# A macaron layer in fp32 on one NeuronCore: the first feed-forward's copies and gates put in another order on ScalarE, row 7 turned a block later where feed-forward and attention meet, and the last block summed in two column halves

## The chip, the core and the metric

The kernel runs on one NeuronCore of a Trainium2 chip. The metric is the device time of one execution in microseconds (us), lower is better. The profile names the engines: PE is TensorE's matmul and PEld its weight load, ACT is ScalarE, DVE is VectorE, POOL is GpSimd, SP is SyncE, whose queue issues nearly all transfers.

## The reference, cut to what matters

The input is x with 1024 rows (tokens) of 1024 columns in fp32. DEPTH is 1, so only the layer with stick-breaking attention is there.

```python
def rms_norm(x, gain):
    y = x * lax.rsqrt(jnp.mean(x * x, axis=-1, keepdims=True) + 1e-6)
    return y * gain

def swiglu(xn, w_in, w_out):             # w_in 1024 x 5632, w_out 2816 x 1024
    gate, up = jnp.split(xn @ w_in, 2, axis=-1)
    return (jax.nn.silu(gate) * up) @ w_out

def reference(x, ...):
    x = x + 0.5 * swiglu(rms_norm(x, n1), w1_in, w1_out)
    x = x + stick_breaking_attention(rms_norm(x, gm), w_qkv, gq, gk, w_o)   # 16 heads of 64
    x = x + 0.5 * swiglu(rms_norm(x, n2), w2_in, w2_out)
    return x
```

## The kernel before, in words

**Split numbers.** Every product of two fp32 matrices is made from two parts of each operand. `split` (L196, L197) makes the high part on ACT by a Copy into fp32r and the low part on DVE or POOL by subtracting it. `mm3` (L308 to L310) then issues three matmuls into the same PSUM bank: high by high, high by low, low by high.

**Feed-forward, up.** `ffn_in` works through eleven pairs q of weight column blocks. A pair has a gate phase and an up phase; in each of them `seven` forms four 128 x 512 results from seven products (a Strassen form) of twelve matmuls each. The products go to the banks `ka`, `kc` and `kb` in the order ka, kc, kb, ka, kc, ka, kb. The bank `ka` is used three times in one phase and each use adds onto what stands there; in between, `copy` (L499, ACT) takes the bank's present content into a tile `s`, so PE may not start the second or the third use before the copy is done. `prepare` makes the seven weight operands of a phase: sums of weight blocks on DVE (`sf`, L475), then the splits by `unit` (tiles `u`), named a11, s1, a12, s2, s4, s3, a22. The operands of a phase are made about a phase ahead. After the gate phase four Silu activations run on ACT in place (`g`, L547), each behind the DVE sum that completes its tile (L503). For q = 2 alone the Silus are ordered behind the split of the gate phase's s3 (`marks["s3"]`, `following`). `following(mark)` only orders instructions of the mark's own engine; it adds no semaphore.

**Feed-forward, down.** `ffn_out` makes the second product from seven sums too, `SEVEN`: the products 5, 1, 4, 3, 7, 2, 6. Each takes four PSUM banks, `ma` or `mb`, one for each block t of 128 rows, and its operands come in six chunks loaded by SP (L361, L364), summed on DVE (L576) and split on ACT, DVE and POOL into tiles `rp`. Completed banks are added onto x on DVE (`result`, L622). The last product, 6, is summed block by block for its last three chunks (fifteen matmuls a block), so that finished rows can be used while PE sums the next block.

**The joint.** In the first feed-forward the blocks of product 6 are where the attention's input is made. `at` is called behind each block. `norm` scales a finished row (a row is 128 tokens here) on DVE into `xs` (L263), `turned` transposes it with eight matmuls of 128 columns into two banks (L287) and splits the two banks into `xh` and `xl`. Rows 4 to 7 are complete before product 6, rows 0 to 3 with its blocks 0 to 3. Behind block 0 the rows 6 and 7 are turned, sixteen matmuls, into mb0 to mb3, the banks of product 2, which DVE has to add onto x first. Row 0 is turned behind block 3, row 1 behind the first row of the QKV projection (bank `bt`, which lies where mb0 and mb1 were), rows 2 and 3 later. The rate of a row (its inverse root mean square) goes ACT square (L239), POOL sum and power (L248, L219, L220), and the row's scalings follow on DVE. Beside this ACT and POOL split the first QKV weights (`wqh`, `wql`, L948, L951). Two small POOL instructions (L946) hold the second half of these weights behind the last row turned, row 7 (`last_x`).

**The end.** The last block of the second feed-forward's product 6 is summed like every other one, added onto x on DVE and stored by SP (L1342).

**Order.** Each engine runs its instructions in the order of its queue. A list scheduler sets that order by the program's order and by the buffers; `following` (`tc.issue_after`) adds a constraint to it.

Of the kernel before, what the change touches and what calls it, by code (L numbers as in the profile page):

```python
# [17 lines left out]
P = 128  # L18
# [95 lines left out]
def macaron_kernel(ctx, tc, x, g1, w1_in, w1_out, gm, w_qkv, gq, gk, w_o, g2, w2_in, w2_out, out):  # L114
# [155 lines left out]
    def turned(xs, tb, bk, tl=None):  # L270
# [13 lines left out]
        for d in range(2):  # L284
# [5 lines left out]
            split(tp, xh[dst], xl[dst])  # L290
# [139 lines left out]
    def ffn_in(pl, w_in, keep, tl, hb, right, last):  # L430
# [35 lines left out]
        def prepare(raw, behind=None):  # L466
# [17 lines left out]
            us["s4"] = unit(pl, f["s4"], pool_e)  # L484
            mix("s3", a11, a21, ALU.subtract)
            us["s3"] = unit(pl, f["s3"], pool_e)
            marks["s3"] = marks["unit"]
# [6 lines left out]
        def seven(us, result):  # L494


            def copy(b):
                s = small(pl, "s")
                act.activation(s, b, AF.Copy)  # L499
                return s  # L500
# [13 lines left out]
            s2 = copy(a)  # L514
            product(c, us["s4"], b22, False)
# [11 lines left out]
        for q in range(1, NQ):  # L527
# [17 lines left out]
            for g in gs.values():  # L545
                with following(marks["s3"] if q == 2 else None):
                    act.activation(g, g, AF.Silu)  # L547

            us = prepare(stream(pl, w_in, q, 1), before[1, 1][:, 0:1] if q == 1 else None)
# [8 lines left out]
    def ffn_out(pl, w_out, keep, x_from, ahead, at):  # L558
# [37 lines left out]
        for m, tag, fresh, goes in SEVEN:  # L596
# [11 lines left out]
            def add(ts, cs):  # L608
                for c in cs:
                    (wh, wl), (hh, hl), _ = ops[c]  # L610
                    for i, q in enumerate(CHUNKS[c]):
                        for t in ts:
                            s = slice(t * P, (t + 1) * P)
                            mm3(
                                bs[t], [((hh[:, i, s], hl[:, i, s]), (wh[:, i], wl[:, i]))],
                                fresh and q == 0, q == NQ - 1, not fresh,
                            )

            def result(t, bs=bs, goes=goes):
                for (th, h), sign in goes:  # L620
                    xc = x_sb[h][:, 4 * (1 - th) + t, :]
                    dve.scalar_tensor_tensor(out=xc, in0=bs[t], scalar=0.5 * sign, in1=xc, op0=ALU.mult, op1=ALU.add)  # L622
# [7 lines left out]
            for t in range(4):  # L630
                add([t], range(n, len(CHUNKS)))
                if not late:
                    result(t)
                if last:
                    at(x_sb, m, f"block {t}", ops)
# [30 lines left out]
    with pools(*RAWS) as pr:  # L666
# [200 lines left out]
        with banks("ps2"), pools(*SECOND) as pl:  # L867
# [4 lines left out]
            def at(x_sb, m, where, ops):  # L872
# [25 lines left out]
                elif m == 6 and str(where).startswith("block"):  # L898
                    t = int(where[-1])
                    turn_rows("mb", (2, 0, 0, 1)[t])  # L900
                    squares(pn, row, (t,), half[:, t : t + 1], (1,))
                    last_norm = lambda: pending.extend(norm(pn, row, (t,), gain_m, half[:, t : t + 1], pooled=True))
                    if t < 3:
                        last_norm()
                    else:
                        late.append(last_norm)
# [9 lines left out]
    with ExitStack() as stack:  # L916
# [239 lines left out]
        last_x = ((pool_e, 0, lambda: xl[:, KD - 1, T - P : T - P + 1].bitcast(F32)),)  # L1156
# [170 lines left out]
    with banks("ps4"), pools(*SECOND) as pl:  # L1327
        lay_banks()

        def at(x_sb, m, where, ops):  # L1330
# [9 lines left out]
            for tb in tbs:  # L1340
                for h in hs:
                    sp.dma_start(out[rows(tb), HALVES[h]], x_sb[h][:, tb, :])  # L1342
# [42 lines left out]
```

## Time and profile before

| what | value |
|---|---|
| three runs | 1914.53, 1916.08, 1917.19 us |
| their median | 1916.08 us |
| the profiled execution | 1914.4 us |
| its span in the trace | 1912.5 us |
| PE busy | 1897.4 us (99%) |
| DVE, POOL, ACT busy | 1237.0, 1127.8, 979.9 us |
| bytes moved by DMA | 258.65 MB |

The span runs from the first to the last instruction of the trace; the time of the same execution is 1.9 us longer. A row of the timeline has the start in us from the span's start, the duration, engine, line, operation, tiles (out<-in), shapes and the count of merged instructions; in brackets stand the idle time before it and what ended that. A matmul's duration overlaps the next one's: the step from one start to the next is what counts on PE. A row of the waits has the waiting instruction, whom it waited for, the sum in us, the number of waits and the longest.

### The profile page before, as it was taken

To read this page: it belongs to the slowest core of one execution; us is meant where nothing else is said; L and a number is where in the kernel's file an instruction comes from. 1 tells how busy PE (TensorE), PEld (TensorE's weight loads), DVE (VectorE), ACT (ScalarE), POOL (GpSimd) and SP (SyncE) were. 2 spreads that over 40 slices of the span, in tenths; PEclk is the share of its full clock that TensorE was granted. 3 is DMA by queue.
4 is the path that set the end of the run, shared out by engine and by line. 5 is a ranking of instruction groups with operands and counts; after the bars stand their busy time and mean duration, and the time that the engine had idled before them with its cause. 6 is when DMAs were issued, how large, how long until landed. Compare 5 with 4: busy or idle time off the path is not lost.

```text
span 1912.5 us, 26698 instructions
## 1 busy us (share of the span) xinstructions
PE 1897.4 (99%) x9362; PEld 1624.8 (85%) x9362; DVE 1237.0 (65%) x1713; ACT 979.9 (51%) x1794; POOL 1127.8 (59%) x999
## 2 busy tenths in 40 slices
PE   9999999999999999999999999999999999999999
PEld 8878888888888899999999897788888888888887
DVE  6856445535775758888888777568456445548645
ACT  7433433334335458878888876344433443434332
POOL 6766666656556746656665564215666666654554
PEclk9999999999999999999999999999999999999999
DMA  6233323338897411011111152612333323369983
GB/s 204 89 115 111 105 87 117 105 115 278 307 354 259 138 34 45 32 47 45 45 37 42 50 170 74 225 50 74 103 110 116 105 83 117 110 229 342 331 268 138
DMA packets 168982, 258.65 MB, mean 135 GB/s; under 512 B 11664, under 2 KB 82320, under 8 KB 168848
## 3 DMA queue, kind: packets, MB, share of 16 engines
q1 hardware_dynamic: 168704, 256.95, 39.3%
q8 instruction: 73, 1.20, 0.3%
q14 instruction: 61, 0.50, 0.1%
q10 hardware_dynamic: 144, 0.00, 0.0%
HBM read 197.14 MB, written 59.77 MB: 134 GB/s over the span
## 4 chain that ended last, share of the span: by engine, by line
PE 86%; DVE 8%; ACT 3%; issue 1%; POOL 1%; DMA 0%; SPq 0%; DVEq 0%; ACTq 0%; POOLq 0%
PE ka L308 6%; PE ka L309 6%; PE ka L310 6%; PE bq L308 4%; PE bq L309 4%; PE bq L310 4%; PE kc L308 4%; PE kc L309 4%; PE kc L310 4%; PE ma L310 4%; PE ma L309 4%; PE ma L308 4%; PE kb L308 4%; PE kb L309 4%; PE kb L310 4%; PE mb L310 3%
## 5 line engine op out<-in xcount | busy, mean ns | idle before, releaser
L197 POOL TENSOR_TENSOR rp<-raw,rp 128x1024 fp32r<-128x1024 f32 x84 | 213.7, 2551 | 168.0 <-ACT rp L196 157.0
L197 POOL TENSOR_TENSOR u<-sf,u 128x512 fp32r<-128x512 f32 x160 | 227.6, 1425 | 136.2 <-ACT u L196 136.2
L197 POOL TENSOR_TENSOR u<-raw,u 128x512 fp32r<-128x512 f32 x128 | 187.5, 1467 | 152.5 <-ACT u L196 151.7
L196 ACT ACTIVATE u<-sf 128x512 fp32r<-128x512 f32 x160 | 100.8, 630 | 204.7 <-PE kb L309 87.1
L1073 POOL TENSOR_TENSOR w<-w,om 128x512 f32<-128x512 f32 (+4 forms) x128 | 140.9, 1104 | 107.6 <-DVE om L1066 94.0
L446 DVE TENSOR_TENSOR h<-h 128x512 f32<-128x512 f32 x110 | 135.4, 1234 | 85.8 <-POOL h L554 85.1
L308 PE MATMUL bq<-wqh,xh 128*128 128x384 f32 x512 | 174.4, 341 | 0.4
L196 ACT ACTIVATE rp<-rh 128x1024 fp32r<-128x1024 f32 (+1 forms) x78 | 76.4, 983 | 189.9 <-issue 60.2
L309 PE MATMUL bq<-wql,xh 128*128 128x384 f32 x512 | 172.2, 336 | 0.0
L310 PE MATMUL bq<-wqh,xl 128*128 128x384 f32 x512 | 172.1, 336 | 0.0
L576 DVE TENSOR_TENSOR raw<-raw 128x1024 f32<-128x1024 f32 (+1 forms) x60 | 95.0, 1585 | 105.4 <-DMA raw<-w_out 91.7
L196 ACT ACTIVATE u<-raw 128x512 fp32r<-128x512 f32 x128 | 80.2, 630 | 149.8 <-PE ka L309 100.8
L308 PE MATMUL ka<-xh,u 128*128 128x512 f32 x352 | 137.2, 390 | 1.9 <-ACT s L499 1.9
L308 PE MATMUL ma<-rp 128*128 128x512 f32 x352 | 137.0, 389 | 0.0
L310 PE MATMUL ka<-xh,u 128*128 128x512 f32 x352 | 137.0, 389 | 0.0
L310 PE MATMUL ma<-rp 128*128 128x512 f32 x352 | 136.9, 389 | 0.0
L309 PE MATMUL ka<-xl,u 128*128 128x512 f32 x352 | 136.9, 389 | 0.0
L309 PE MATMUL ma<-rp 128*128 128x512 f32 x352 | 136.9, 389 | 0.0
L554 POOL TENSOR_TENSOR h<-h,g 128x512 f32<-128x512 f32 x80 | 113.0, 1412 | 35.1 <-DVE h L503 33.3
L1062 ACT ACTIVATE w<-bz,f 128x512 f32<-128x512 f32 (+1 forms) x192 | 113.1, 589 | 34.5 <-PE bz L1058 33.4
L475 DVE TENSOR_TENSOR sf<-raw 128x512 f32<-128x512 f32 x80 | 80.3, 1003 | 77.9 <-POOL u L197 77.9
L197 DVE TENSOR_TENSOR rp<-rh,rp 128x1024 fp32r<-128x1024 f32 (+1 forms) x70 | 109.7, 1585 | 21.9 <-ACT rp L196 19.6
(309 smaller groups left out, 5465.8 us busy)
## 6 DMA issues: line engine op xcount, KB each, us to landing
raw<-w_out SPq DMA_DIRECT2D x120, 512.0 KB, 5.7
raw<-w_in SPq DMA_DIRECT2D x86, 512.0 KB, 3.6
k<-h SPq DMA_DIRECT2D x154, 256.0 KB, 2.1
rh<-k SPq DMA_DIRECT2D x64, 512.0 KB, 6.2
raw_qkv<-w_qkv SPq DMA_DIRECT2D x64, 192.0 KB, 2.9
x_keep<-x SPq DMA_DIRECT2D x32, 256.0 KB, 3.4
x<-x_keep SPq DMA_DIRECT2D x32, 256.0 KB, 5.6
raw<-w_out SPq DMA_DIRECT2D x24, 256.0 KB, 4.6
```

Of the source, the lines that this page charges most:

```text
L196: first = act.activation(hi, raw, AF.Copy).ins
L197: return first, (engine or dve).tensor_tensor(lo, raw, hi.bitcast(F32), op=ALU.subtract).ins
L308: pe.matmul(dst, ah, bh, start=start and i == 0, stop=False, skip_group_check=onto)
L309: pe.matmul(dst, ah, bl, start=False, stop=False, skip_group_check=onto)
L310: pe.matmul(dst, al, bh, start=False, stop=stop and i == n - 1, skip_group_check=onto)
L446: dve.tensor_tensor(src, hb[of[0]], hb[of[1]], op=getattr(ALU, of[2]))
L475: dve.tensor_tensor(f[n], x, y, op=op)
L554: pool_e.tensor_tensor(h, h, gs[k], op=ALU.mult)
L576: dve.tensor_tensor(w[0], w[0], w[1], op=getattr(ALU, W_OF[m][2]))
L1062: marks["scored"] = act.activation(to, z, AF.Sigmoid, scale=state["f", half][:, sign, tb % 4, hd : hd + 1]).ins
L1073: marks["weighed"] = pool_e.tensor_tensor(wt[:, c1 : c0 + n], wt[:, c1 : c0 + n], om[:, c1 - 1 : c0 + n - 1], op=ALU.mult).ins
```

## The change

There are four edits.

1. In `ffn_in`, the up phase of q = 1: the split of s4 is ordered behind the gate phase's copy of the second use of `ka` (`marks["s2"]`).
2. In `ffn_in`, q = 2: the four Silus are ordered behind the same copy of their own gate phase, and no longer behind the split of s3.
3. At the joint: behind block 0 only row 6 is turned and row 7 behind block 1. The scalings of row 1 are ordered behind the sum of block 2, those of row 2 behind the split of row 0. The weights' marker reads row 6 in place of row 7.
4. In the second feed-forward, the last block is summed, added and stored in two halves of 256 columns.

`ffn_in` and its edits are shared by both feed-forwards.

```diff
@@ turned
-            split(tp, xh[dst], xl[dst])
+            marks["turned"] = split(tp, xh[dst], xl[dst])[1]
@@ ffn_in
-        def prepare(raw, behind=None):
+        def prepare(raw, behind=None, copied=None):
...
-            us["s4"] = unit(pl, f["s4"], pool_e)
+            with following(copied):
+                us["s4"] = unit(pl, f["s4"], pool_e)
...
-            marks["s3"] = marks["unit"]
...
             s2 = copy(a)
+            marks["s2"] = marks["copy"]
...
-                with following(marks["s3"] if q == 2 else None):
+                with following(marks["s2"] if q == 2 else None):
                     act.activation(g, g, AF.Silu)
...
-            us = prepare(stream(pl, w_in, q, 1), before[1, 1][:, 0:1] if q == 1 else None)
+            us = prepare(
+                stream(pl, w_in, q, 1), *((before[1, 1][:, 0:1], marks["s2"]) if q == 1 else ())
+            )
@@ ffn_out
             for t in range(4):
-                add([t], range(n, len(CHUNKS)))
-                if not late:
-                    result(t)
-                if last:
-                    at(x_sb, m, f"block {t}", ops)
+                for part in parts if last and t == 3 else (slice(0, NHALF),):
+                    add([t], range(n, len(CHUNKS)), part)
+                    if not late:
+                        result(t, n=part)
+                    if last:
+                        at(x_sb, m, f"block {t}", ops, part)
@@ at, first feed-forward
-                    turn_rows("mb", (2, 0, 0, 1)[t])
+                    turn_rows("mb", (1, 1, 0, 1)[t])
                     squares(pn, row, (t,), half[:, t : t + 1], (1,))
-                    last_norm = lambda: pending.extend(norm(pn, row, (t,), gain_m, half[:, t : t + 1], pooled=True))
-                    if t < 3:
-                        last_norm()
+                    rate = partial(rates, pn, row, (t,), half[:, t : t + 1], True)
+                    if t == 0:
+                        pending.extend(norm(pn, row, (0,), gain_m, r=rate()))
+                    elif t < 3:
+                        late.append(rate())
+                        if t == 2:
+                            pending.extend(norm(pn, row, (1,), gain_m, r=late.pop(0), behind=marks["result"]))
                     else:
-                        late.append(last_norm)
+                        pending.extend(norm(pn, row, (2,), gain_m, r=late.pop(), behind=marks["turned"]))
+                        late.append(lambda: pending.extend(norm(pn, row, (3,), gain_m, r=rate())))
@@ the weights' marker
-        last_x = ((pool_e, 0, lambda: xl[:, KD - 1, T - P : T - P + 1].bitcast(F32)),)
+        last_x = ((pool_e, 0, lambda: xl[:, KD - 1, T - 2 * P : T - 2 * P + 1].bitcast(F32)),)
@@ at, second feed-forward
-                    sp.dma_start(out[rows(tb), HALVES[h]], x_sb[h][:, tb, :])
-        ffn_out(pl | pr, w2_out, keep, x_keep[1], ops, at)
+                    sp.dma_start(out[rows(tb), HALVES[h]][:, part], x_sb[h][:, tb, part])
+        ffn_out(pl | pr, w2_out, keep, x_keep[1], ops, at, [slice(n, n + NHALF // 2) for n in (0, NHALF // 2)])
```

ACT's queue before, in the first feed-forward at the gate phase of q = 2. The tile g_1307 is that phase's first gate tile, s_1321 the copy of the second use of its bank ka0, and u_1404 the split of the up phase's s3:

```order
L499 ACTIVATE s_1292<-kc1_1265 128x512
L196 ACTIVATE u_1398<-sf_1396 128x512
L547 ACTIVATE g_1307<-g_1307 128x512
L196 ACTIVATE u_1404<-sf_1402 128x512
L499 ACTIVATE s_1321<-ka0_1264 128x512
L196 ACTIVATE u_1408<-raw_1373 128x512
```

The same place after the change:

```order
L499 ACTIVATE s_1292<-kc1_1265 128x512
L196 ACTIVATE u_1398<-sf_1396 128x512
L196 ACTIVATE u_1404<-sf_1402 128x512
L499 ACTIVATE s_1321<-ka0_1264 128x512
L548 ACTIVATE g_1307<-g_1307 128x512
L196 ACTIVATE u_1408<-raw_1373 128x512
```

The Silu has moved from two places ahead of the copy to the place behind it. One pair earlier, at q = 1, it is a split: the split of sf_1081 (s4 of the up phase) stood two places ahead of the copy s_982 and stands one behind it now; POOL's two subtractions for s4 and s3 of that phase have changed places with it.

DVE's queue before, at the joint, from the sum of block 0 to the first reduction of the QKV projection. The rows with x1 and ma0 to ma3 are the sums of the blocks 0 to 3; xs_5841, xs_5868 and xs_5895 are the scaled rows 0, 1 and 2; the rows with xl and mb are the splits of a turned row:

```order
L622 SCALAR_TENSOR_TENSOR x1_4176<-ma0_5601,x1_4176 128x512
L197 TENSOR_TENSOR xl_67<-mb1_5812,xh_66 128x4x128
L197 TENSOR_TENSOR xl_67<-mb3_5826,xh_66 128x4x128
L263 SCALAR_TENSOR_TENSOR xs_5841<-x1_4176,rs_y_5838,gain_4172 128x512
L622 SCALAR_TENSOR_TENSOR x1_4176<-ma1_5602,x1_4176 128x512
L263 SCALAR_TENSOR_TENSOR xs_5868<-x1_4176,rs_y_5865,gain_4172 128x512
L622 SCALAR_TENSOR_TENSOR x1_4176<-ma2_5603,x1_4176 128x512
L622 SCALAR_TENSOR_TENSOR x1_4176<-ma3_5604,x1_4176 128x512
L263 SCALAR_TENSOR_TENSOR xs_5895<-x1_4176,rs_y_5892,gain_4172 128x512
L197 TENSOR_TENSOR xl_67<-mb1_5921,xh_66 128x4x128
```

The same place after the change (of each pair of splits and of scalings the second one is shown, here and above):

```order
L627 SCALAR_TENSOR_TENSOR x1_4176<-ma0_5601,x1_4176 128x512
L197 TENSOR_TENSOR xl_67<-mb1_5812,xh_66 128x4x128
L263 SCALAR_TENSOR_TENSOR xs_5827<-x1_4176,rs_y_5824,gain_4172 128x512
L627 SCALAR_TENSOR_TENSOR x1_4176<-ma1_5602,x1_4176 128x512
L197 TENSOR_TENSOR xl_67<-mb3_5853,xh_66 128x4x128
L627 SCALAR_TENSOR_TENSOR x1_4176<-ma2_5603,x1_4176 128x512
L263 SCALAR_TENSOR_TENSOR xs_5892<-x1_4176,rs_y_5865,gain_4172 128x512
L627 SCALAR_TENSOR_TENSOR x1_4176<-ma3_5604,x1_4176 128x512
L197 TENSOR_TENSOR xl_67<-mb1_5918,xh_66 128x4x128
L263 SCALAR_TENSOR_TENSOR xs_5927<-x1_4176,rs_y_5889,gain_4172 128x512
```

The split of row 7 (mb3) stands behind the sum of block 1, the scalings of row 1 stand behind the sum of block 2, and those of row 2 behind the split of row 0 (the last mb1). ACT's two second weight splits and the square of row 0 now stand ahead of row 7's split. On PE the eight matmuls that turn row 7 have moved from the front of block 1 to the front of block 2, and the last block's fifteen matmuls of 512 columns have become thirty of 256. POOL's order at the joint is unchanged.

More of the change, by code (lines that the diff above doesn't have):

```diff
@@ L498, in copy @@
                 s = small(pl, "s")
-                act.activation(s, b, AF.Copy)
+                marks["copy"] = act.activation(s, b, AF.Copy).ins
                 return s
@@ L556, in ffn_in, with ffn_out @@
         more.close()
-    def ffn_out(pl, w_out, keep, x_from, ahead, at):
+    def ffn_out(pl, w_out, keep, x_from, ahead, at, parts=(slice(0, NHALF),)):
         place["rp"] = 0
@@ L606, in ffn_out, with add @@
                     loaded.add((th, h))
-            def add(ts, cs):
+            ends = CHUNKS[-BY_BLOCK - 1][-1] if last and len(parts) > 1 else NQ - 1
+            def add(ts, cs, n=slice(0, NHALF)):
                 for c in cs:
@@ L614, in add, with result @@
                             mm3(
-                                bs[t], [((hh[:, i, s], hl[:, i, s]), (wh[:, i], wl[:, i]))],
-                                fresh and q == 0, q == NQ - 1, not fresh,
+                                bs[t][:, n], [((hh[:, i, s], hl[:, i, s]), (wh[:, i, n], wl[:, i, n]))],
+                                fresh and q == 0, q == NQ - 1 or (t == 3 and q == ends), not fresh or n != slice(0, NHALF),
                             )
-            def result(t, bs=bs, goes=goes):
+            def result(t, bs=bs, goes=goes, n=slice(0, NHALF)):
                 for (th, h), sign in goes:
-                    xc = x_sb[h][:, 4 * (1 - th) + t, :]
-                    dve.scalar_tensor_tensor(out=xc, in0=bs[t], scalar=0.5 * sign, in1=xc, op0=ALU.mult, op1=ALU.add)
+                    xc = x_sb[h][:, 4 * (1 - th) + t, n]
+                    marks["result"] = dve.scalar_tensor_tensor(
+                        out=xc, in0=bs[t][:, n], scalar=0.5 * sign, in1=xc, op0=ALU.mult, op1=ALU.add
+                    ).ins
             n = len(CHUNKS) - BY_BLOCK if last else len(CHUNKS)
@@ L870, in macaron_kernel, with at @@
             half = pn["xs"].tile([P, 4, 2], F32, name="half", bufs=1)
-            def at(x_sb, m, where, ops):
+            def at(x_sb, m, where, ops, part=None):
                 def row(tb, h):
@@ L1328, in macaron_kernel, with at @@
         lay_banks()
-        def at(x_sb, m, where, ops):
+        def at(x_sb, m, where, ops, part=slice(0, NHALF)):
             tbs, hs = (), ()
```

## The prediction

> **What bounds the kernel now.** I read the page first, then PE's waits, then the timelines around the longest of them.
>
> ```profile
> PE 1897.4 (99%) x9362; PEld 1624.8 (85%) x9362; DVE 1237.0 (65%) x1713; ACT 979.9 (51%) x1794; POOL 1127.8 (59%) x999
> ```
>
> PE is busy for 99% of the span. No other engine exceeds 65%. The change takes no matmul away, so all that it can win is idle time of PE and the tail behind PE's last matmul. The waits of PE, longest first, with total, number and longest:
>
> ```profile
> PE ka L308 <- ACT s L499: 1.9, 2, 1.4
> ...
> PE mb L287 <- DVE x L622: 0.9, 2, 0.5
> ...
> PE bt L287 <- DVE xl L197: 0.5, 1, 0.5
> ```
>
> The edits reach the three rows shown: the two waits for a copy (first feed-forward), the two for mb and the one for bt (joint). They add up to 3.3 us as the profile counts idle time; what a wait costs in steps between starts is more, as shown below. The rows left out (start-up, attention) are not touched.
>
> **First feed-forward, the two copies.** PE and ACT at the first wait:
>
> ```profile
> 74.62 1.15 ACT L196 ACTIVATE u<-sf 128x512 fp32r<-128x512 f32 x2 [2.26 <-DVE sf L475]
> 75.68 0.58 ACT L499 ACTIVATE s<-ka 128x512 f32<-128x512 f32 x1
> ...
> 75.48 0.39 PE L310 MATMUL kc<-xh,u 128*128 128x512 f32 x1
> 76.31 0.50 PE L308 MATMUL ka<-xh,u 128*128 128x512 f32 x1 [0.44 <-ACT s L499]
> 79.17 0.39 PE L308 MATMUL kb<-t3h,u 128*128 128x512 f32 x1
> ```
>
> The copy ends at 76.26 and PE goes on at 76.31, so the copy is what it waited for. The copy stood behind two splits, and the first of them, s4's, waited 2.26 us for its sum on DVE. The sum of the second, s3's, was done long before:
>
> ```profile
> 71.05 1.78 DVE L475 TENSOR_TENSOR sf<-raw 128x512 f32<-128x512 f32 x1
> ```
>
> Without s4 ahead of it, ACT has s3's split (its sum is done at 72.83) and then the copy, from about 73.5; it ends by about 74.1, 1.6 us ahead of PE. The step from one 512-column matmul to the next is 0.227 us (the last block below: 14 steps in 3.17 us), so PE would have started ka at 75.71 in place of 76.31: 0.60 us. The block behind the wait also runs slowly: twelve matmuls take 2.86 us (76.31 to 79.17) where twelve steps are 2.72, another 0.14 us. The second wait, a pair later:
>
> ```profile
> 114.45 0.63 ACT L547 ACTIVATE g<-g 128x512 f32<-128x512 f32 x1 [4.76 <-DVE g L503]
> 115.51 0.58 ACT L499 ACTIVATE s<-ka 128x512 f32<-128x512 f32 x1
> ...
> 111.58 0.39 PE L310 MATMUL ka<-t1h,u 128*128 128x512 f32 x1
> 116.14 0.50 PE L308 MATMUL ka<-xh,u 128*128 128x512 f32 x1 [1.45 <-ACT s L499]
> 119.02 0.39 PE L308 MATMUL kb<-t3h,u 128*128 128x512 f32 x1
> ```
>
> The bank was complete at 111.97 (111.58 + 0.39), but ACT stood 4.76 us at a Silu that waited for DVE, and then ran another split. Behind the change only a split is left ahead of the copy, so the copy ends at about 113, 1.5 us early. PE, after the twelve matmuls of kc, would have started ka 13 steps behind 111.58, at 114.53; it gains 116.14 - 114.53 = 1.61, and 2.88 - 2.72 = 0.16 behind it. What is moved costs nothing here: the Silu waits for DVE's sum until 114.42 wherever it stands, and s4's split is needed by PE a phase later. Sum for this feed-forward: 0.60 + 0.14 + 1.61 + 0.16 = 2.5 us. The second feed-forward gets the same order and had no such wait: nothing.
>
> **The joint.** PE from the last matmul of block 0 on, and DVE beside it:
>
> ```profile
> 646.44 1.03 PE L287 MATMUL mb<-ident,xs 128*128 128x128 f32 x8
> 647.86 0.65 PE L287 MATMUL mb<-ident,xs 128*128 128x128 f32 x4 [0.39 <-DVE x L622]
> 649.06 0.66 PE L287 MATMUL mb<-ident,xs 128*128 128x128 f32 x4 [0.54 <-DVE x L622]
> 649.47 0.48 PE L308 MATMUL ma<-rp 128*128 128x512 f32 x1
> 660.58 0.42 PE L308 MATMUL bq<-wqh,xh 128*128 128x384 f32 x1
> 664.67 0.34 PE L310 MATMUL bq<-wqh,xl 128*128 128x384 f32 x1
> 665.54 1.22 PE L287 MATMUL bt<-ident,xs 128*128 128x128 f32 x8 [0.53 <-DVE xl L197]
> 666.52 0.42 PE L308 MATMUL bq<-wqh,xh 128*128 128x384 f32 x1
> ...
> 644.14 4.86 DVE L622 SCALAR_TENSOR_TENSOR x<-mb,x 128x512 f32<-128x512 f32 x8
> 659.33 1.42 DVE L263 SCALAR_TENSOR_TENSOR xs<-x,rs_y,gain 128x512 f32<-128x512 f32 x2 [4.31 <-POOL rs_y L220]
> 660.66 1.28 DVE L622 SCALAR_TENSOR_TENSOR x<-ma,x 128x512 f32<-128x512 f32 x2
> 664.71 1.28 DVE L197 TENSOR_TENSOR xl<-mb,xh 128x512 fp32r<-128x512 f32 x2
> ```
>
> Eight transposes that wait for nothing step by 0.11 us, 0.87 in all. Row 6's eight start at 646.44 and meet free banks. Row 7's need mb2 and mb3, which DVE's eight sums release at 647.8 and 649.0: block 1 could start at 646.44 + 16 x 0.109 = 648.18 and starts at 649.47, so 1.29 us are lost. Moved behind block 1 (fifteen steps, 3.4 us), row 7 meets banks that have long been free. Row 1's eight start at 665.54, because DVE splits row 0 only at 664.71, behind the sums of the blocks 2 and 3, which stood 4.31 us behind a rate, and behind row 2's scalings. PE could have gone on at 664.84 (0.17 a step): 0.70, and its eight take 0.98 until 666.52 in place of 0.87: 0.11. Sum: 2.1 us.
>
> What is late next? Row 0's split is now behind the sum of block 3 and row 1's scalings. I follow it in the times of before: row 0's square on ACT comes about 1.0 us earlier, since row 7's two of the four splits (half of 2.04) no longer stand ahead of it, and so do POOL's rate and everything behind it:
>
> ```profile
> 649.13 2.04 ACT L196 ACTIVATE xh<-mb 128x512 fp32r<-128x512 f32 x4
> ...
> 654.10 4.12 POOL L951 TENSOR_TENSOR wql<-raw_qkv,wqh 128x384 fp32r<-128x384 f32 x4 [0.28 <-ACT wqh L948]
> 658.74 0.56 POOL L220 TENSOR_TENSOR rs_y<-rs_a,power 128x1 f32<-128x1 f32 x1
> ```
>
> Row 1's rate ends near 658.3 in place of 659.30, its scalings near 659.8 (+1.42), the sum of block 3 near 660.4, row 0's splits near 661.7 (+1.28). PE then comes to row 1 at 664.84 - 1.29 = 663.55, a cushion of 1.9 us. The first QKV weights are split by 657.2, PE needs them from 659.3. The moved marker costs POOL nothing: row 6 is split before it is reached.
>
> **The tail.** The last block, the sum behind it and the store; then a run of 24 matmuls of 256 columns from the chain of waits, and a 256-column sum:
>
> ```profile
> 1905.04 0.39 PE L308 MATMUL ma<-rp 128*128 128x512 f32 x1
> 1908.21 0.39 PE L310 MATMUL ma<-rp 128*128 128x512 f32 x1
> 1908.64 0.69 DVE L622 SCALAR_TENSOR_TENSOR x<-ma,x 128x512 f32<-128x512 f32 x1 [2.71 <-PE ma L310]
> DMA to landing us min/median/max: 2.0/2.0/2.0
> ...
> 27.94 2.88 PE kc L324 x24
> L762 DVE SCALAR_TENSOR_TENSOR xl<-kb,g_sb,xh x24: 473/474/751, 9.7 to 42.2; 128x256 fp32r<-128x256 f32 x16, 128x512 fp32r<-128x512 f32 x8
> ```
>
> A 256-column matmul steps by 0.12 us, more than half of 0.227: thirty take 3.60 in place of fifteen in 3.40, so +0.2. The last sum shrinks from 0.69 to between 0.42 and 0.47 (of the L762 rows the 512-column ones take 0.75, the 256-column ones 0.47), -0.25. The last store carries 128 KB in place of 256 KB; no store of that size is in the trace. Its saving lies between 0 (2.0 us whatever the size) and 1.0 (half of it); the 256 KB stores land in the same 2.0 whether alone or not far apart, so I stay near the lower end and take 0.25. Sum: 0.3 us gained, with ends of 0 and 1.05.
>
> The Trainium skill, page "DMA: Bandwidth & Descriptors", section "Anatomy of one DMA — SWDGE (gpsimd) path", speaks against the halves: a transfer costs about 2.0 us whatever it carries, plus its bytes by 436 GB/s. By that rule the estimate of the store's saving is 0.3 us and the tail's sum 0.35. The trace does not agree on the size, since 256 KB would take 2.6 us by the rule and 2.0 were measured; that the fixed part dominates cannot be told from it.
>
> **The sum** is 2.5 + 2.1 + 0.3 = 4.9 us, made against the profiled execution's own time: 1914.4 - 4.9 = 1909.5 us. That execution lies 1.7 below the median of the runs, 1916.08, and the same 4.9 us put the median at 1911.2 us. What a measurement of this kernel can tell from no change is about 0.2%, 3.8 us, so the forecast stands 1.1 us beyond it.
>
> **The rivals.** First: the first feed-forward's gain is given back in its second product. There PE runs close behind operands that wait for loads:
>
> ```profile
> 507.10 2.84 DVE L576 TENSOR_TENSOR raw<-raw 128x1024 f32<-128x1024 f32 x1 [1.52 <-DMA raw<-w_out]
> 514.64 2.34 DVE L197 TENSOR_TENSOR rp<-rh,rp 128x1024 fp32r<-128x1024 f32 x2
> 516.14 0.39 PE L308 MATMUL ma<-rp 128*128 128x512 f32 x1
> ```
>
> The split for PE's chunk at 516.14 is done at 515.85 (half of 2.34 after 514.64), 0.3 us ahead, at the end of a DVE chain that starts with a landed load. If those loads land when they did, PE arrives 2.5 us early and waits: the gain is 2.4 us, 1913.7. Against it speaks that the loads are issued when tiles come free behind PE's own matmuls, so they move up with it. Chance 0.17.
>
> Second: the joint gives half back, since one of the moved instructions is late: the fourth of DVE's eight sums ends only 0.3 us before row 6's second bank needs it (644.14 plus half of 4.86, against 646.44 plus four steps), and the cushion for row 1 is worked out by hand. Gain near 3.8 us, 1912.3. Chance 0.12.
>
> Third, slower: the chain behind row 0's rate (weight splits, POOL's four subtractions, row 1's rate and scalings, the sum of block 3, row 0's splits) becomes what PE waits for at row 1. DVE slows where POOL works beside it:
>
> ```profile
> 639.42 4.80 DVE L263 SCALAR_TENSOR_TENSOR xs<-x,rs_y,gain 128x512 f32<-128x512 f32 x4
> ```
>
> Four scalings took 4.80 us, two at 659.33 took 1.42, so a pair can cost 1.0 more. PE waits from 1.9 us of lateness on; the whole gain is gone at 1.9 + 4.9 = 6.8, and at 8 the kernel is 1.2 slower, 1917.3. It would take several such pairs and a late rate as well. Chance 0.04.
>
> Fourth: the order is changed but the copy is not what frees PE at the first wait (s3's split may itself be late there). Then 0.74 is missing: 1911.9. Chance 0.05.
>
> **How the numbers follow.** Forecast 0.62, rivals 0.17, 0.12, 0.04, 0.05. The forecast's own ends are the tail's (4.6 to 5.65 us), and the runs before spread by 1.5 us to either side of their median. From 1911.2 less 0.75 and 1.1 of spread I set the low end at 1909.4; the high end holds the first rival with 0.7 of spread, 1914.4. Faster by over 0.2%: most of the forecast (0.53 of 0.62, the rest lost to spread) and some of the second and fourth rival, 0.60. Within 0.2%: 0.37, the first rival above all. Slower by over 0.2%: 0.03.
>
> **What would show it.** In the new trace the row of ka waiting for s should be gone, both rows of mb and bt too; the copies should end near 74.1 and 112.3, PE should reach the transposes behind block 0 at about 643.9 and the second QKV row at about 661.9, and the last matmul, 256 columns wide, should end 4.4 us earlier (2.5 + 2.1, less the 0.2 that the halves cost). The forecast is wrong if PE waits anew for rp tiles between 450 and 646, for mb or bt at the joint, or if the last store takes longer than 2.0 us.

## The result and the profile after

The changed kernel takes 1910.0 us, median of 11 runs (1909.55 to 1911.73); the kernel before, on the same chip, 1914.94 us (11 runs, 1914.24 to 1917.19). The ratio is 0.9973, with a 95% interval from 0.9964 to 0.9982: 4.9 us by the medians, 3.4 to 6.9 by the interval. The forecast was 4.9 us and 1911.2 us. The time came out 1.2 us below that, nearly all of it because the forecast was taken from a median of three runs of the kernel before (1916.08), where eleven give 1914.94. The profiled execution took 1910.43 us with a span of 1908.3 us, 4.2 us below the span before.

The engines' busy time, from the page of the changed kernel:

```profile
PE 1897.0 (99%) x9377; PEld 1626.1 (85%) x9377; DVE 1236.2 (65%) x1714; ACT 979.4 (51%) x1794; POOL 1128.8 (59%) x999
```

PE is busy for as long as before (1897.4), with 15 matmuls more. So what was gained is idle time of PE. The waits of PE in the changed kernel:

```profile
PE ma L308 <- DVE x L627: 0.5, 1, 0.5
...
PE mb L287 <- DVE x L627: 0.2, 1, 0.2
```

The row of ka waiting for a copy is gone, and so is the row of bt. Of the two waits of mb one is left, and it has moved: it is row 6's now, as shown below. The row of ma is new. L627 is the sum that was L622, so PE now waits for a sum of the last block.

To see where the time went, I compare the start of the same matmul in both traces. Up to each of these six, both PE programs hold the same number of matmuls (row 7's transposes stand elsewhere between the third and the fourth, but are in both). First before, from PE's timeline (start, length, engine, line, operation):

```profile
13.89 0.28 PE L324 MATMUL ka<-xl,u 128*128 128x256 f32 x1
144.86 0.39 PE L308 MATMUL kc<-t0h,u 128*128 128x512 f32 x1
630.34 0.39 PE L309 MATMUL ma<-rp 128*128 128x512 f32 x1
680.52 0.33 PE L308 MATMUL bq<-wqh,xh 128*128 128x384 f32 x1
1263.10 0.39 PE L310 MATMUL bt<-wi,xl 128*128 128x512 f32 x1
1901.19 0.39 PE L309 MATMUL ma<-rp 128*128 128x512 f32 x1
```

Then the changed kernel:

```profile
14.57 0.28 PE L324 MATMUL ka<-xl,u 128*128 128x256 f32 x1
143.07 0.39 PE L308 MATMUL kc<-t0h,u 128*128 128x512 f32 x1
628.56 0.39 PE L309 MATMUL ma<-rp 128*128 128x512 f32 x1
676.87 0.33 PE L308 MATMUL bq<-wqh,xh 128*128 128x384 f32 x1
1258.73 0.39 PE L310 MATMUL bt<-wi,xl 128*128 128x512 f32 x1
1896.84 0.39 PE L309 MATMUL ma<-rp 128*128 128x512 f32 x1
```

PE is 0.68 us late at the first row, 1.79 early at the second, 1.78 at the third, 3.65 at the fourth, 4.37 at the fifth and 4.35 at the last. The differences from row to row are the stages: opening +0.68, the two waits of the first feed-forward -2.46 (with unrounded starts), the rest of that feed-forward 0.00, joint -1.87, attention -0.71, second feed-forward +0.02. What is left to the span's difference of 4.20 is the tail: it became 0.14 us **longer**. The same table for every experiment stands behind the experiments.

Two of these stages, the opening and the attention, hold no compute instruction that the change moves. The opening is eighteen matmuls on the cleared xl. The kernel before, then the changed one, PE's timeline:

```profile
1.64 6.06 PE L691 MATMUL kc<-xl 128*128 128x512 f32 x18 [1.64 <-POOL xl L685]
```

```profile
1.64 6.97 PE L699 MATMUL kc<-xl 128*128 128x512 f32 x18 [1.64 <-POOL xl L693]
```

The same eighteen took 6.06 and 6.97 us. They are not the whole of this stage: with row 7 alone (below) they took 5.91 us, and the opening was still 0.65 us late, because `ka` (L324) then waited 0.7 us for a split of DVE. So part of a span's difference is luck of one execution, and stages have to be compared, not spans.

**First feed-forward.** ACT and PE at the two places:

```profile
74.23 0.58 ACT L499 ACTIVATE s<-ka 128x512 f32<-128x512 f32 x1
76.39 0.39 PE L308 MATMUL ka<-xh,u 128*128 128x512 f32 x1
112.31 0.58 ACT L499 ACTIVATE s<-ka 128x512 f32<-128x512 f32 x1
114.52 0.39 PE L308 MATMUL ka<-xh,u 128*128 128x512 f32 x1
116.04 0.63 ACT L548 ACTIVATE g<-g 128x512 f32<-128x512 f32 x1 [3.15 <-DVE g L503]
```

The copies end at 74.81 and 112.89, some 1.6 us ahead of PE, and neither ka row has an idle time behind it. The Silu (L548) still waits 3.15 us for DVE, but now nothing that PE needs stands behind it.

**The joint.** DVE and PE:

```profile
630.20 2.98 DVE L579 TENSOR_TENSOR raw<-raw 128x1024 f32<-128x1024 f32 x1 [5.09 <-DMA raw<-w_out]
642.90 4.86 DVE L627 SCALAR_TENSOR_TENSOR x<-mb,x 128x512 f32<-128x512 f32 x8
645.43 0.66 PE L287 MATMUL mb<-ident,xs 128*128 128x128 f32 x4 [0.17 <-DVE x L627]
645.84 0.48 PE L308 MATMUL ma<-rp 128*128 128x512 f32 x1
659.05 1.28 DVE L197 TENSOR_TENSOR xl<-mb,xh 128x512 fp32r<-128x512 f32 x2
662.09 0.27 PE L287 MATMUL bt<-ident,xs 128*128 128x128 f32 x1
```

Row 0's splits end at 660.33 and PE comes to row 1 at 662.09: that wait is gone, with a cushion of 1.76 us. But the eight sums start at 642.90, only 1.24 us earlier than before (644.14), while PE is 1.78 earlier. So the second four of row 6's transposes wait for mb1. DVE works without a break from the first row on, and that row starts when a load lands; in the kernel before, the same instruction started earlier although PE was later:

```profile
629.05 3.14 DVE L576 TENSOR_TENSOR raw<-raw 128x1024 f32<-128x1024 f32 x1 [2.55 <-DMA raw<-w_out]
```

**The tail.** PE, DVE, the last store and the stores' landing times:

```profile
1902.37 0.28 PE L310 MATMUL ma<-rp 128*128 128x256 f32 x1
1902.68 0.42 DVE L627 SCALAR_TENSOR_TENSOR x<-ma,x 128x256 f32<-128x256 f32 x1 [1.10 <-PE ma L310]
1903.16 0.39 PE L308 MATMUL ma<-rp 128*128 128x256 f32 x1 [0.52 <-DVE x L627]
1904.93 0.28 PE L310 MATMUL ma<-rp 128*128 128x256 f32 x1
1905.25 0.42 DVE L627 SCALAR_TENSOR_TENSOR x<-ma,x 128x256 f32<-128x256 f32 x1 [2.14 <-PE ma L310]
...
out<-x SPq DMA_DIRECT2D x1, 256.0 KB, 2.0
out<-x SPq DMA_DIRECT2D x2, 128.0 KB, 1.7
```

The second half's first matmul would follow the first half's last by 0.12 us, at 1902.49. It starts at 1903.16, when DVE has read the first half (1902.68 + 0.42 = 1903.10), though the two halves share no column. That is 0.67 us, and the first step behind it takes 0.1 us longer than the others: 0.77 in all. The sum (0.42 for 0.69) and the store (1.7 for 2.0) are shorter by what was forecast, 0.27 and 0.3.

### The profile page after: what moved, and what is told of

Its sections match the earlier page's. It is cut to its first block, busy times and chain, and to the rows that moved or that the text cites. A ratio compares the mean times of both kernels' runs of the same rounds, so it can differ in the third digit from the quotient of the medians.

```text
span 1908.3 us, 26722 instructions
## 1 busy us (share of the span) xinstructions
PE 1897.0 (99%) x9377; PEld 1626.1 (85%) x9377; DVE 1236.2 (65%) x1714; ACT 979.4 (51%) x1794; POOL 1128.8 (59%) x999
## 4 chain that ended last, share of the span: by engine, by line
PE 88%; DVE 6%; ACT 4%; issue 1%; POOL 1%; DMA 0%; ACTq 0%; DVEq 0%; POOLq 0%
PE ka L309 6%; PE ka L308 6%; PE ka L310 6%; PE kc L309 4%; PE kc L308 4%; PE kc L310 4%; PE ma L308 4%; PE ma L310 4%; PE ma L309 4%; PE kb L309 4%; PE kb L308 4%; PE kb L310 4%; PE bq L308 4%; PE bq L309 4%; PE bq L310 4%; PE mb L310 3%
## 5 line engine op out<-in xcount | busy, mean ns | idle before, releaser
L579 DVE TENSOR_TENSOR raw<-raw 128x1024 f32<-128x1024 f32 (+1 forms) x60 | 90.8, 1516 | 109.0 <-DMA raw<-w_out 92.6
L308 PE MATMUL ma<-rp 128*128 128x512 f32 (+1 forms) x357 | 138.1, 387 | 0.5 <-DVE x L627 0.5
L309 PE MATMUL ma<-rp 128*128 128x512 f32 (+1 forms) x357 | 137.8, 386 | 0.0
L310 PE MATMUL ma<-rp 128*128 128x512 f32 (+1 forms) x357 | 137.8, 386 | 0.0
```

The lines of the kernel that those rows point to most:

```text
L308: pe.matmul(dst, ah, bh, start=start and i == 0, stop=False, skip_group_check=onto)
L309: pe.matmul(dst, ah, bl, start=False, stop=False, skip_group_check=onto)
L310: pe.matmul(dst, al, bh, start=False, stop=stop and i == n - 1, skip_group_check=onto)
L579: dve.tensor_tensor(w[0], w[0], w[1], op=getattr(ALU, W_OF[m][2]))
```

## The experiments

My theory, A: each gain was made where a wait of PE stood, and stays there but for what the next late engine takes back; the tail's halves lose, because both lie in one bank. Its rivals: the first feed-forward's gain is mostly paid back before or at the joint (B); at the first wait it was not the copy (C); row 0's chain is late at row 1 (D); the tail is as the prediction had it, without a wait (P). "Before" in each result is the kernel before on the same chip.

**The feed-forwards' edits alone.** On the kernel before:

```diff
-            us["s4"] = unit(pl, f["s4"], pool_e)
+            with following(copied):
+                us["s4"] = unit(pl, f["s4"], pool_e)
...
-                with following(marks["s3"] if q == 2 else None):
+                with following(marks["s2"] if q == 2 else None):
                     act.activation(g, g, AF.Silu)
...
```

> Only the two edits of the feed-forwards (the s4 split and the Silu put behind a bank's copy), on the kernel before. Theory A (each gain is made where a wait of PE stood, and stays, less what the next late engine takes back): both waits on the copies are gone, PE is 2.4 us earlier from 119 us to 640 us, and at the joint DVE's eight sums have come only about 1.9 us earlier, so that 0.5 us goes back at row 7's transposes, which wait longer; span about 1.9 us shorter, time about 1913.0 against 1914.9. Rival B (the gain is mostly paid back before or at the joint): less than 1.0 us remains, time above 1913.9. Rival C (the copy was not what freed PE at the first wait): PE is 1.7 us earlier at 640 us in place of 2.4.

Measured: 1912.1 us against 1914.66, ratio 0.9987 (0.9978 to 0.9996). PE's waits at the joint:

```profile
PE mb L287 <- DVE x L626: 1.3, 3, 0.5
```

There were two such waits before, of 0.9 us in all; now there are three, and the joint takes back 0.53 us of the 2.46 gained. That is A's mechanism and, in this profile, its size. The time fell by more than A said (2.6 for 1.9), which one median of this spread does not contradict. B and C are out: both waits on the copies are gone and 2.46 us are there at 144 and at 630 us.

**Only the Silu's edit**, with the s4 split left where it was:

> Of the feed-forwards' edits only the Silu of the second pair put behind the copy, on the kernel before. Theory A (each wait stands by itself): the wait at 116 us (1.61 and 0.16) goes, that at 76 us (0.74) stays, and PE is 1.8 us earlier from 120 us on; 0.2 to 0.5 us of it goes back at the joint, where DVE comes later; gain 1.3 to 1.8, time 1912.9 to 1913.4. Rival C (at the first wait it was not the copy): all of the feed-forwards' gain is here, 2.5 us, time about 1912.2.

Measured: 1912.74 us against 1914.96, ratio 0.9988 (0.9979 to 0.9997). PE at the two places:

```profile
76.25 0.50 PE L308 MATMUL ka<-xh,u 128*128 128x512 f32 x1 [0.43 <-ACT s L499]
114.46 0.39 PE L308 MATMUL ka<-xh,u 128*128 128x512 f32 x1
```

The first wait stays, the second is gone, and the stage gains 1.78 us; the rest of the 2.46 is the first wait's, 0.68 (forecast: 1.77 and 0.74). C falls again. A's further claim, that 0.2 to 0.5 us would go back at the joint, missed: there the stage differs by 0.01, since DVE's sums came 1.84 us earlier, as PE did. DVE's run from the load to the sums started at 627.2 us here and at 629.6 with both edits. So the joint takes something back only where that load is late for PE. It does not hang on the edits alone: the run with the last block whole, below, holds both edits and loses nothing there. Why the load is late in one profile and not in another was not tried.

**The joint's edits alone**, on the kernel before:

```diff
-                    turn_rows("mb", (2, 0, 0, 1)[t])
+                    turn_rows("mb", (1, 1, 0, 1)[t])
...
-                    if t < 3:
-                        last_norm()
+                    elif t < 3:
+                        late.append(rate())
+                        if t == 2:
+                            pending.extend(norm(pn, row, (1,), gain_m, r=late.pop(0), behind=marks["result"]))
...
-                        late.append(last_norm)
+                        pending.extend(norm(pn, row, (2,), gain_m, r=late.pop(), behind=marks["turned"]))
...
-        last_x = ((pool_e, 0, lambda: xl[:, KD - 1, T - P : T - P + 1].bitcast(F32)),)
+        last_x = ((pool_e, 0, lambda: xl[:, KD - 1, T - 2 * P : T - 2 * P + 1].bitcast(F32)),)
```

> Only the joint's edits (row 7 turned a block later, its marker, scalings behind the sums), on the kernel before. Theory A: the waits of the transposes on DVE at 647 to 649 us and at 665.5 us are gone, 1.29 and 0.76 us, without the new 0.33 us at row 6 that the changed kernel has, since PE does not come early: 2.0 us, time about 1912.9 against 1914.9. Rival B (the joint is the place where the feed-forward's gain is let through, and has little of its own): under 1.0 us, time above 1913.9. Rival D (the chain behind row 0's rate becomes late at row 1): a wait at row 1's transposes longer than the 0.70 us of before, gain 1.3 us or less.

Measured: 1911.86 us against 1914.66, ratio 0.9985 (0.9976 to 0.9994). No wait of mb or bt of that kind is left in the list, and the joint gains 2.23 us: A. B and D are out.

**Row 7 alone**, and **the scalings alone**, each on the kernel before. The one keeps the third edit above and the first, the other only the middle one.

> Of the joint's edits only row 7's turn a block later, with its marker, on the kernel before; the scalings keep their order. Theory A (two waits that stand by themselves): the 1.29 us at row 7 are gained, the wait at row 1 (0.70 us before) grows by 0.2 to 0.4 us, because row 0's chain comes about 1.0 us earlier and PE 1.3; gain about 1.0 us, time about 1913.7. Rival (row 0's chain does not move with it, and row 1 takes it all back): the wait at row 1 is about 2.0 us, gain under 0.3 us.

> Of the joint's edits only the order of the scalings and sums, on the kernel before; row 7 is turned where it was. Theory A: the waits at row 7 stay (1.29 us), the wait at row 1 (0.76 us in all) goes, and a second-row cushion of about 1 us is left; gain 0.8 us, time about 1913.9 against 1914.7. Rival (the scalings are worth what is missing from the joint's 2.8 once row 7 alone has given 0.8): 1.8 us or more, 1912.9.

Row 7 alone: 1913.94 us against 1914.78, ratio 0.9994 (0.9986 to 1.0003). The transposes at 647 to 649 us wait no more, but PE then stands longer at row 1:

```profile
665.60 0.30 PE L287 MATMUL bt<-ident,xs 128*128 128x128 f32 x1 [1.09 <-DVE xl L197]
```

The idle time was 0.53 us and is 1.09: of the 1.29 won, the stage keeps 0.56. A's mechanism, but not its size (1.0): the wait grew by 0.56 and not by 0.2 to 0.4, because row 0's chain came only 0.6 us earlier with row 7 out of its way, not 1.0 (with the 0.62 us taken off by which this whole profile is late there). That would leave 0.73; the other 0.17 went at row 6, whose eight transposes took 1.00 us to the next matmul (647.06 to 648.06) where row 7's took 0.79. DVE's sums, behind a late load, came 0.98 us later than before, PE 0.62.

The scalings alone: 1912.98 us against 1914.96, ratio 0.9992 (0.9983 to 1.0001). Their time, 2.0 us below, would speak for the rival, but its interval holds 0.9 as well, so the trace has to decide. The one at row 1 is gone from PE's waits, the two at row 7 are as they were, and the joint gains 0.91 us, as A has it:

```profile
PE mb L287 <- DVE x L622: 0.9, 2, 0.5
```

The rest of that time's difference lies in the attention, -0.57 in this profile, where nothing was moved. Apart, the two edits give 0.56 and 0.91; together 2.23. The scalings' order is worth 0.9 by itself and 1.7 behind row 7's move, because it also clears the wait that the move makes longer.

**How near row 1 is to being late.** The changed kernel with `behind=marks["turned"]` taken from row 2's scalings:

> The changed kernel with one of its orders undone: DVE scales row 2 (1.4 us) ahead of row 0's splits again. This asks how far the changed kernel is from the slower case of the prediction, in which row 0's chain comes late at row 1. Theory A (row 0's splits end 1.8 us ahead of PE): the splits come 1.4 us later and PE still does not wait; time as the changed kernel, 1909.9 to 1910.2. Rival (the chain is already the bound at row 1): PE waits 0.5 to 1.4 us there, time 1910.6 or more.

Measured: 1910.37 us against 1914.96, ratio 0.9976 (0.9967 to 0.9986). Row 0's splits and row 1's first transpose:

```profile
659.71 1.28 DVE L197 TENSOR_TENSOR xl<-mb,xh 128x512 fp32r<-128x512 f32 x2
662.13 0.49 PE L287 MATMUL bt<-ident,xs 128*128 128x128 f32 x3
```

Only one of row 2's two scalings came ahead of the splits, so they end at 660.99, 0.66 us later than in the changed kernel and not the 1.4 expected. PE still does not wait; 1.14 us of cushion are left. The test was half as strong as meant, and within that D's condition is not met.

**The last block in halves, alone**, on the kernel before (loop over `parts`, two sums, two stores):

> Only the last block in halves, on the kernel before. Theory A (the second half waits for the first half's sum, because both lie in one bank): PE stops for about 0.65 us in the middle of the block, so the last matmul is 1.0 us later than it would be, the sum is 0.27 shorter and the store 0.5 us shorter: between 0.1 us faster and 0.3 us slower, time 1914.8 to 1915.2. Theory P (the prediction's: no such wait, PE loses 0.2, sum and store give 0.5): 0.3 us faster, 1914.6, and no gap between the halves.

Measured: 1915.22 us against 1914.66, ratio 1.0004 (0.9996 to 1.0013); by time alone unclear. In the trace the gap between the halves is there (an idle 0.52 us for x L624 in PE's waits), and the tail is 0.44 us longer than before. The halves cost, as A says, though 0.44 is more than the 0.3 it allowed; P is out.

**The changed kernel again, with its last block whole, and with a bank for the second half**, three runs on one chip. The bank's edit:

```diff
+                    own = bank("mb") if part.start else None
-                    add([t], range(n, len(CHUNKS)), part)
+                    add([t], range(n, len(CHUNKS)), part, own)
...
-                        result(t, n=part)
+                        result(t, n=part if own is not None or part.stop == NHALF else slice(0, NHALF), own=own)
```

`add` then writes the second half into `own`, starting from zero, and `result` reads it from there; the first sum takes all 512 columns of ma, so that the second half's earlier chunks are added too.

> The changed kernel, with the last 15 matmuls of the last block's second half put into a bank of their own; the first sum takes all 512 columns of the first bank (0.69 us in place of 0.42), the last one the 256 columns of the new bank. Theory A (the shared bank is what makes PE wait): no gap between the halves, the last matmul, sum and store are 0.65 to 0.75 us earlier, time 0.7 us below the changed kernel, about 1909.3. Theory P (the gap is the first half's own length or comes of the switch to a new group of matmuls): a gap stays, time as the changed kernel, 1910.0.

> The changed kernel once more, on the chip on which the next three run, so that they can be compared with it: 4.9 us below the kernel before, about 1909.8, and the two waits that the change brought (row 6's transposes about 0.3 us, the second half of the last block about 0.65 us) in its trace again.

> The second half of the last block in a bank of its own once more, since its times lay in two groups. Theory A (PE's wait on the shared bank is on the path that sets the end): 0.5 to 0.8 us below the changed kernel of the same chip. Rival: the end is set by something behind the last store that starts no earlier; then 0.2 us below it or less although the last sum is 0.75 us earlier.

> The changed kernel with its last block whole again (512 columns, one sum, one store). Theory A (halves in one bank lose about 0.35 us): 0.1 to 0.5 us below the changed kernel of the same chip. Theory P (halves gain 0.3 us): 0.3 us above it.

The bank's first run (with the three of the feed-forwards, the joint and the tail): 1909.93 us against 1914.66, ratio 0.9976 (0.9966 to 0.9985), by time no different from the changed kernel. The three on one chip, before at 1914.78: changed kernel again 1910.17, ratio 0.9976 (0.9966 to 0.9986); own bank 1909.52, 0.997 (0.9959 to 0.9982); whole 1909.82, 0.9974 (0.9963 to 0.9984). The order is A's, the differences (0.65 and 0.35 us) have its size, and the intervals overlap, so the traces have to carry it. In the changed kernel's second trace both new waits are there again (0.2 us idle for mb, 0.5 for ma). The own bank's first run:

```profile
1901.86 0.28 PE L310 MATMUL ma<-rp 128*128 128x256 f32 x1
1901.98 0.28 PE L308 MATMUL mb<-rp 128*128 128x256 f32 x1
1903.66 0.28 PE L310 MATMUL mb<-rp 128*128 128x256 f32 x1
1903.98 0.42 DVE L627 SCALAR_TENSOR_TENSOR x<-mb,x 128x256 f32<-128x256 f32 x1 [1.10 <-PE mb L310]
```

The second half follows by one step, 0.12 us, and the block's thirty matmuls start within 3.47 us in place of 4.24 (1900.19 to 1903.66, 1900.69 to 1904.93). The block whole:

```profile
1903.70 0.39 PE L310 MATMUL ma<-rp 128*128 128x512 f32 x1
1904.13 0.69 DVE L627 SCALAR_TENSOR_TENSOR x<-ma,x 128x512 f32<-128x512 f32 x1 [2.71 <-PE ma L310]
```

The same run shows that the wait at row 6 is not a fixed price of putting the edits together. It has the changed kernel's joint, and yet no transposes wait, for the load landed early enough and the sums came 1.88 us earlier than before, as PE did:

```profile
628.00 2.32 DVE L579 TENSOR_TENSOR raw<-raw 128x1024 f32<-128x1024 f32 x1 [3.37 <-DMA raw<-w_out]
642.27 4.86 DVE L627 SCALAR_TENSOR_TENSOR x<-mb,x 128x512 f32<-128x512 f32 x8
```

From the start of the last block to the end of the span, against before: halves in one bank +0.14 to +0.16 (the changed kernel twice and the run on row 2's scalings), whole -0.30, halves in two banks -0.61 and -0.62. P and the rival that something behind the last store sets the end are both out. (A whole block gave -0.30 or 0.00, halves in one bank 0.15 or 0.44: two values each, 0.3 apart, as described at the end. I compare the lower with the lower: 0.45 between halves and whole. The upper ones differ by 0.44. The own bank's three are of the lower kind: 2.66 to 2.68 us from the last sum to the end, as in the changed kernel.) The new bank is also a new tile of the program, so these runs do not tell whether the bank or the program's order by tiles makes PE wait.

**Both new waits taken away.** The own bank, and row 6 turned with row 7 behind block 1:

```diff
-                    turn_rows("mb", (1, 1, 0, 1)[t])
+                    turn_rows("mb", (0, 2, 0, 1)[t])
...
-        last_x = ((pool_e, 0, lambda: xl[:, KD - 1, T - 2 * P : T - 2 * P + 1].bitcast(F32)),)
+        last_x = ((pool_e, 0, lambda: stores[0].args[0](0, 1)[:, 0:1]),)
```

> The changed kernel with both of its new waits taken away: the last half block in a bank of its own, and row 6 turned with row 7 behind block 1, where its banks are long free; the marker of the QKV weights' splits is put on the sum of block 0, since it hung on row 6's split. Theory A: no wait at row 6's transposes (0.25 to 0.4 us), none in the last block (0.65); about 1.0 us below the changed kernel, 1909.1. Rival (DVE then has four splits between the sums and row 0's chain comes late at row 1): a new wait at row 1, no more than the own bank's gain, 1909.5 or above.

Measured: 1909.16 us against 1914.96, ratio 0.997 (0.9959 to 0.9981), the lowest median of all kernels here, 1.2 us below the run on row 2's scalings, on the same chip. No transposes wait at the joint, which gains 2.27 us. How much of that the new place of row 6 gives is not shown: in this profile the sums came 2.60 us earlier and PE 2.61, so row 6 would hardly have waited at its old place either, and the run with the last block whole gains 2.23 there without this edit. Row 1 is not late:

```profile
658.37 1.27 DVE L197 TENSOR_TENSOR xl<-mb,xh 128x512 fp32r<-128x512 f32 x2
660.88 0.49 PE L287 MATMUL bt<-ident,xs 128*128 128x128 f32 x3
```

The stages of all profiles, as differences to the profile before, in us, worked out as for the changed kernel above (the rest of the first feed-forward, 145 to 630 us, is 0.00 or -0.01 everywhere and left out; negative is faster):

| kernel | opening | first FF | joint | attention | second FF | tail | span |
|---|---|---|---|---|---|---|---|
| changed | 0.68 | -2.46 | -1.87 | -0.71 | 0.02 | 0.14 | -4.20 |
| changed, again | -0.08 | -2.46 | -1.76 | -0.31 | 0.01 | 0.16 | -4.44 |
| feed-forwards' edits | -0.18 | -2.46 | 0.53 | -0.39 | 0.57 | -0.30 | -2.21 |
| only the Silu | -0.05 | -1.78 | -0.01 | -0.29 | 0.00 | 0.00 | -2.13 |
| joint's edits | -0.14 | 0.02 | -2.23 | -0.59 | 0.01 | 0.01 | -2.93 |
| only row 7 | 0.65 | -0.03 | -0.56 | 0.07 | 0.02 | -0.01 | 0.15 |
| only the scalings | -0.04 | -0.03 | -0.91 | -0.57 | 0.00 | -0.01 | -1.57 |
| only the halves | -0.06 | 0.03 | -0.03 | -0.06 | 0.02 | 0.44 | 0.34 |
| row 2 undone | 0.58 | -2.51 | -1.69 | -0.29 | 0.00 | 0.15 | -3.76 |
| own bank | -0.03 | -2.49 | -1.84 | -0.51 | 0.02 | -0.61 | -5.47 |
| own bank, again | 0.27 | -2.51 | -1.74 | 0.06 | 0.01 | -0.62 | -4.56 |
| last block whole | 0.58 | -2.46 | -2.23 | -0.42 | 0.02 | -0.30 | -4.81 |
| both waits away | -0.14 | -2.47 | -2.27 | 0.41 | 0.00 | -0.62 | -5.07 |

## Why the prediction was right, and where it was not

**First feed-forward, 2.5 us forecast:** 2.46 in the trace, 0.68 and 1.78 for the two waits (0.74 and 1.77 forecast). The copies end at 74.81 and 112.89, where 74.1 and about 113 were named (112.3 among the signs); the profile's opening is 0.68 us late, and without it the first is 74.13. Every step on PE's path held. One beside it did not: the Silu's sum on DVE was to end at 114.42 wherever the Silu stands and ended at 116.01, which cost PE nothing.

**Joint, 2.1 us forecast:** 2.23 when it is alone, 1.87 and 1.76 behind the first feed-forward's gain. The two waits were sized rightly. What was missing is that DVE's sums can stay behind when PE comes early. The prediction named the spot in its second rival, "the fourth of DVE's eight sums ends only 0.3 us before row 6's second bank needs it", but took the sums to move up with PE. In the changed kernel they did so by 1.24 us of 1.78, behind a load that landed at 630.2 us. It cost 0.4 us of the joint's gain, not the half that the rival put down, and nothing in the run with the last block whole, where the load came early. A new wait for mb at the joint stands among the signs of being wrong; this one sign came up, with 0.17 us idle.

**Row 0's chain:** a cushion of 1.9 us at row 1 was forecast; 1.76 were measured. With one of row 2's scalings put back ahead of the splits, 1.14 us remained. The rival that would have made the kernel slower never came near.

**Tail, 0.3 us gain forecast:** this step failed. The prediction wrote "thirty take 3.60 in place of fifteen in 3.40, so +0.2", as if they ran without a break. The halves are two of one bank's columns, and PE's first matmul of the second half waits until DVE has read the first: 0.77 us more. Halves in one bank lose 0.44 us against the block as a whole (0.14 against -0.30 in the table), where 0.3 gained was forecast: this term was off by 0.74. So the last matmul ended 3.39 us earlier (1908.60 to 1905.21) and not 4.4. With the wait taken away by a second bank they win 0.32 us against it (-0.62 against -0.30), which is the forecast's term. So the sizes of matmul, sum and store were right; the wait was not seen. The Trainium skill has the rule that would have shown it: the page "PSUM — Partial Sum Buffer", section "PSUM bank collisions raise a hardware error", has TensorE's writes and VectorE's reads of a bank kept apart by bank and quadrant, not by address. The trace agrees, in that PE was held until the reading was over; no kernel was tried here in which both work on one bank at once.

**First rival, loads behind the second product of the first feed-forward:** it did not come there (0.00 between 145 and 630 us in every profile with this edit). Its mechanism was seen at two other places: at the joint, as said, and once in the second feed-forward, where the feed-forwards' edits alone lost 0.57 us to a split of DVE. Other kernels, 4 us early at the same place, did not, so it looks like one execution's.

**The sum.** In the changed kernel's profile the edits give 2.46 + 1.87 - 0.14 = 4.19 us, not 4.9. The span's 4.20 agrees with that only because 0.68 of bad luck in the opening and 0.71 in the attention cancel. The medians say 4.9 and 4.6 with intervals of about 1.8 us to either side. So the forecast's total is nearer to the medians than to its own terms: against this profile 0.44 was mis-sized in the tail and 0.23 at the joint. That its tail is not worse is luck too: the kernel before was profiled with the longer of its two ends, the changed one with the shorter. With like ends the edits come to 3.9 us. That the total was met within 0.1 us is therefore partly luck. Whether the 0.3 to 0.7 us by which most profiles run faster through the attention belong to the change stays open: the own bank's two profiles of one kernel gave -0.51 and 0.06, the halves alone -0.06, the scalings alone -0.57, both waits away 0.41. All these are differences to a single profile of the kernel before.

## What to carry to other kernels

Cutting the last block to start its sum early paid here only with the parts in different banks (0.32 us won, 0.44 lost in one): two parts of one bank went to and fro between PE and the engine that read. A copy or an activation that frees a bank belongs ahead of whatever its engine would wait for; the gain of such an edit can be read off the trace before as the start of PE's next block less the step of a matmul. Where a change gains well under 1% in several places, compare the starts of the same instruction stage by stage, because single spans of one program differ by as much as an edit is worth.

## What the runs showed of the hardware

The eighteen matmuls of the opening took 6.06 us before, 6.97 in the changed kernel and 7.27 in the run on row 2's scalings, with the same instructions and a granted clock of 1.00 in the profile's rows from 0 to 8 us. They step by 0.43 us at first and by 0.23 later, and the moment of the change differs from run to run: some 3.6, 5.7 and 6.5 us after the first start. The Trainium skill, page "TensorE: Matmul & The Clock Gate", section "Part 1: The HAM clock gate", states this: the array runs at half pace until some 4 us of activity, give or take 0.5 from run to run. The steps agree with half pace. The spread of the moment is wider here than that, and the measurement decides; the clock in the rows does not show the change.

From the end of the last sum to the end of the span it took 3.21 us before (1909.33 to 1912.54) and 2.91 with the block whole (1904.82 to 1907.73), with the same store of 256 KB; the two kernels with a store of 128 KB on one bank took 2.67 (changed) and 2.96 (halves alone). So each kind of tail has two values, 0.3 us apart. They do not come from the store, which landed after 2.0 us in both of the former and after 1.7 in both of the latter; the 0.3 us lie behind its landing, and nothing here explains them. A tail's edit worth 0.3 us is therefore seen in one span only by chance.

A wait costs PE more than its idle time: behind the wait of 0.52 us in the last block the second half started 0.67 us late, and the next step took 0.1 us longer than 0.12.
